# Places modulo 256 bytes: weights at four by turns, normed activations and their sums at three

## The chip, the cores and the metric

The kernel runs on one core of one Trainium2 chip, as one program. The metric is the device time of that program in microseconds, as the median of repeated runs; beside it stands one execution that was recorded instruction by instruction, and everything below that is called a profile or a trace comes from that execution. Times of single instructions are given in nanoseconds (ns).

## The reference

The model is a trunk of two identical layers on one sequence of 512 tokens with 1024 features, in float32:

```python
for l in range(DEPTH):                       # DEPTH = 2
    h = rms_norm(x, ln1[l])
    x = x + mixer_block(h, ...)              # one projection w_in for everything below, then
                                             # four causal mixers, sigmoid gates, w_up_*, w_out
    h = rms_norm(x, ln2[l])
    x = x + swiglu(h, w_ffn_in[l], w_ffn_out[l])

def swiglu(h, w_in, w_out):
    gate, up = jnp.split(h @ w_in, 2, axis=-1)
    return (jax.nn.silu(gate) * up) @ w_out  # 2816 hidden features
```

Nearly all of the arithmetic is in the dense products: the combined projection `w_in`, the four `w_up`, `w_out`, and the two of the feed-forward part. The mixers (forgetting attention, gated linear attention, retention, a state-space scan) work on 64-wide heads and are small beside them.

## The kernel before

**Layout.** Activations are kept transposed: 128 features on the partitions, 512 tokens along a partition, eight such blocks for 1024 features. A product is built of blocks of 128 x 128 weights: the weight block is the stationary operand of a matmul (it is loaded into the array by a weight load, PEld in the profile), the 512 tokens are the moving operand.

**Two parts of every number.** TensorE multiplies a rounded float32 format in one pass. To keep the precision, each operand is split: `split` (lines 210 and 211) lets ScalarE make the rounded part `hi` and VectorE the remainder `lo`. A product of two split operands is three matmuls, hi.hi, hi.lo and lo.hi (`mm3`). So a weight exists as two tiles, `wh` and `wl`; a normed activation as `xh` and `xl` (class `Norm`); what else is projected from is split into tiles named `t` (mixers' outputs, the merged branches) and `f` (the feed-forward activations).

**The weights' stream.** The weights come in slabs of eight blocks (128 x 1024 float32, 512 KB), in the order in which they are used. `load` fetches a slab into a tile `wr` (two buffers), `convert` splits it into `wh` and `wl` (three buffers each), two slabs ahead of their use (`AHEAD`). `half(tag, shift)` makes such a tile 64 elements longer than the data and returns the data's part from element `shift` on. In the stream `shift` is 16 elements, 64 bytes, for every slab. One slab of eight blocks feeds 24 matmuls.

**The feed-forward input product.** Two of its 22 hidden blocks go through the plain way (`group`). The other 20 go in pairs through a seven-product scheme for 2 x 2 blocks (`strassen`), ten pairs (units) per layer, seven products each, 24 matmuls of 256 tokens per product, so 2 x 10 x 7 x 24 = 3,360 matmuls in all. It needs sums and differences of weights and of activations. The weights' sums are made per unit by VectorE from four slabs (`rq`, and one `wr`), split into `wh` and into a tile `l` of its own pool (or, for three of the products, `wl`, made by an accumulating DMA on line 1278). Here `half` is called with `shift` 0. The activations' sums `t1`, `t2`, `t3` stand in six tiles of pool `tq`; a fourth sum and the three plain quarters stand in the tiles of the second norm, `xh` and `xl`. Partial results are kept in tiles `e` (ScalarE copies them out of the accumulators on line 1340, VectorE adds them on line 1344).

**Order.** The order of the instructions on each engine is fixed when the program is built. The change leaves that order as it is on all five engines.

**Places.** A tile's address along the partition, modulo 256 bytes, is called its place here. Pads between the pools set it. In the program as built, the operands of the large groups of matmuls stand at these places:

| matmuls | moving operand, place | stationary operand, place |
|---|---|---|
| 512 tokens, from a norm (2,976 matmuls) | `xh`, `xl`: 192 | `wh`, `wl`: 192 |
| 512 tokens, from `f` (1,056) and `t` (864) | 192 | `wh`, `wl`: 192 |
| 512 tokens, constants (88) | `t`: 192 | `cr`: 128 |
| 256 tokens, seven-product scheme (3,360) | `xh`, `xl`, `t1`, `t2`, `t3`: 192 | `wh`, `wl`, `l`: 128 |
| 256 tokens, values by tokens (384) | `wh`, `wl`: 192 | `xh`, `xl`: 192 |
| 284 tokens, the wide columns (192) | `wh`, `wl`: 192, 48, 160 | `xh`, `xl`: 192 |

The functions that the change touches, and what calls them:

Of the kernel before, what the change touches and what calls it, by code (L numbers as in the profile page):

```python
# [11 lines left out]
F32R = mybir.dt.float32r  # L12
# [6 lines left out]
P = 128  # L19
S = 512  # L20
D = 1024
KD = D // P
# [13 lines left out]
SLAB = 8  # L36
# [11 lines left out]
HK = KD // 2  # L48
H = S // 2
# [82 lines left out]
def trunk(ctx: ExitStack, tc: tile.TileContext, keys, qkeys, xin, pos, wst, wsq, par, ext, cst, out):  # L132
# [7 lines left out]
    bp = ctx.enter_context(tc.tile_pool(name="bp", bufs=1))  # L140
# [7 lines left out]
    def nm(s):  # L148
        uid[0] += 1
        return f"{s}{uid[0]}"  # L150

    def pad(pool, n):
        pool.tile([P, n // 4], F32, tag=nm("pad"), name=nm("pad"))

    def half(tag, shift):
        t = wp.tile([P, SLAB * P + 64], F32R, tag=tag, name=nm(tag))
        return t[:, shift:shift + SLAB * P]

    pools = {}

    def phase(**bufs):
        if not pools:
            for g, n in zip(gap, (192, 64)):
                pad(g, n)
        st = ExitStack()
        pad(st.enter_context(tc.tile_pool(name=nm("gap"), bufs=1)), 64)
        for n, b in bufs.items():
            pools[n] = st.enter_context(tc.tile_pool(name=nm(n), bufs=b, reuse_waits="tile"))
        return st

    def mixers():
        return phase(gp=2, vp=2, bd=1, tp=33)
# [7 lines left out]
    def FT(shape, dtype=F32):  # L180
        return pools["fp"].tile(shape, dtype, tag="f", name=nm("f"))
# [27 lines left out]
    def split(src, hi, lo):  # L209
        A.copy(out=hi, in_=src)  # L210
        V.tensor_tensor(out=lo, in0=src, in1=hi.bitcast(F32), op=ALU.subtract)  # L211
        return hi, lo
# [38 lines left out]
    def halves(n):  # L251
        w = SLAB * P
        return [slice(0, w // 2), slice(w // 2, w)] if n < 2 else [slice(0, w)]

    def convert():
        n = len(ready)
        if n < SLABS:
            hi, lo = half("wh", 16), half("wl", 16)
            for h in halves(n):
                split(raw[n][:, h], hi[:, h], lo[:, h])  # L260
            ready.append((hi, lo))
            raw[n] = None

    def ahead(n):
        while len(ready) < min(SLABS, cap[0], n):
            if len(raw) == len(ready):
                load()
            convert()
# [24 lines left out]
    scope = mixers()  # L293
# [73 lines left out]
    def rstd_of(total, width):  # L367
# [3 lines left out]
        newton(r, total, width, NT())  # L371
        return r

    class Norm:
        def __init__(self, gain):
            self.gain = gain
            self.hi = bp.tile([P, KD, S], F32R, tag="xh", name=nm("xh"))
            self.lo = bp.tile([P, KD, S], F32R, tag="xl", name=nm("xl"))
            self.part = []

        def __getitem__(self, k):
# [51 lines left out]
    def layer(l, n1, scope):  # L433
# [769 lines left out]
        scope.close()  # L1203


        scope = phase(tq=1, ep=8, rp=5, g0=1, lp=2, g1=1, fp=9)
        pad(pools["g0"], 192)
        pad(pools["g1"], 64)

        last = l == DEPTH - 1  # L1210
        tb_ = {n: tuple(pools["tq"].tile([P, HK, H], F32R, tag=n + h, name=nm(n + h)) for h in "hl") for n in ("t1", "t2", "t3")}
        tb_["t4"] = n2.hi[:, :HK, H:], n2.lo[:, :HK, H:]
        tb_["b11"] = n2.hi[:, :HK, :H], n2.lo[:, :HK, :H]
        tb_["b21"] = n2.hi[:, HK:, :H], n2.lo[:, HK:, :H]
# [29 lines left out]
        def strassen(units):  # L1244
            n = len(units)
            st = [{} for _ in units]
            stream = [(0, 1), (0, 2)]
# [7 lines left out]
            def load(u):  # L1255
                for q, (dk, dm) in (("11", (0, 0)), ("12", (HK, 0)), ("21", (0, 1)), ("22", (HK, 1))):
                    if q == "22":
                        t = wp.tile([P, SLAB * P], F32, tag="wr", name=nm("wr"), bufs=2)
                    else:
                        t = pools["rp"].tile([P, SLAB * P], F32, tag="rq", name=nm("rq"))  # L1260
                    j = len(qkeys) // SLAB
                    for base in (0, FFN):
                        qkeys.extend([("w_ffn_in", l, k + dk, base + (units[u] + dm) * P) for k in range(HK)])
                    nc.sync.dma_start(out=t, in_=wsq[j])
                    st[u][q] = t, j

            def sub(o, a, b, op=ALU.subtract):
                V.tensor_tensor(out=o, in0=a, in1=b, op=op)
                return o

            def LT():
                return pools["lp"].tile([P, SLAB * P], F32R, tag="l", name=nm("l"))

            def early(u, p):
                t, j = st[u][OF[p]]
                lo = half("wl", 0)
                A.activation(out=lo, in_=t, func=AF.Copy, scale=-1.0)  # L1277
                G.dma_start(out=lo, in_=wsq[j], accum_op=ALU.add)  # L1278
                st[u]["lo", p] = lo

            def prep(u, p):
                s = st[u]
                hi = half("wh", 0)
                if p in LATE:
                    A.copy(out=hi, in_=s[OF[p]][0])
                    s[p] = hi, s.pop(("lo", p))
                    return
                a11, a12, a21, a22 = (s[q][0] for q in ("11", "12", "21", "22"))
                if p == 6:
                    s1 = wp.tile([P, SLAB * P], F32, tag="wr", name=nm("wr"), bufs=2)  # L1290
                    s["s1"] = sub(s1, a21, a22, ALU.add)
                    sub(a21, a11, a21)
                    sub(a11, s1, a11)
                    s[p] = split(a11, hi, LT())
                    if u + 1 < len(units):
                        load(u + 1)
                    return
                if p == 3:
                    sub(a12, a12, a11)
                t = {5: s["s1"], 7: a21, 3: a12}[p]  # L1300
                s[p] = split(t, hi, LT())

            done_ = {"early": 0, "prep": 0}

# [7 lines left out]
            def begin(i):  # L1312
                if i < 0:
                    if not done_["early"]:
                        load(0)
                    upto("early", -i, early, lambda p: p in LATE)
                    return
                upto("prep", i + 3, prep, lambda p: True)
                upto("early", i + 6, early, lambda p: p in LATE)
# [74 lines left out]
        a, u = FT([P, 2, S]), FT([P, 2, S])  # L1394
# [5 lines left out]
        hi, lo = split(a, FT([P, 2, S], F32R), FT([P, 2, S], F32R))  # L1400
# [46 lines left out]
    for l in range(DEPTH):  # L1447
        n1 = layer(l, n1, scope if l == 0 else mixers())
# [71 lines left out]
```

## Time and profile before

| what | value |
|---|---|
| median of 3 runs | 1731.86 us (1731.65 to 1731.87) |
| the profiled execution, its own time | 1730.43 us |
| its span, first to last instruction | 1728.7 us |
| TensorE matmuls, busy | 1718.3 us, 99% of the span |
| weight loads, busy | 1497.1 us, 87% |
| VectorE | 1212.5 us, 70% |
| ScalarE | 861.3 us, 50% |
| GpSimd | 227.7 us, 13% |
| DMA engines, mean busy | 20% to 60% by stage, 113 GB/s over the span |
| TensorE clock granted | 0.999 of full speed |

A matmul's duration in the trace runs from its start to its modelled end and overlaps the next one's: a matmul of 512 tokens is shown with about 390 ns while the next one starts some 227 ns after it. So the distance between two starts is what counts, and a difference in the mean duration of two groups of the same size is a difference in that distance. The weight load of the next matmul starts a few ns after a matmul's start and runs beside it.

### The profile page before, as it was taken

The numbers are of one execution on the slowest core, as the hardware profiler recorded it, in microseconds if no ns is written. First come the engines' busy times: TensorE is split into PE (matmuls) and PEld (weight loads), VectorE is DVE, ScalarE is ACT, GpSimd is POOL, SyncE is SP. The second block draws the span as 40 slices with busy tenths as digits, with TensorE's granted clock in tenths as the row PEclk, the third lists the DMA queues.
The fourth block names the chain that finished last, engine by engine and source line by source line (L and its number), as shares of the span: only waits on it lengthen the run. The fifth ranks groups of instructions, "written<-read, shape, count | busy, mean of one in ns | idle before, by whom it ended". The sixth has DMA issues, their size and how long they took to land.

```text
span 1728.7 us, 25141 instructions
## 1 busy us (share of the span) xinstructions
PE 1718.3 (99%) x10140; PEld 1497.1 (87%) x10140; DVE 1212.5 (70%) x1683; ACT 861.3 (50%) x1190; POOL 227.7 (13%) x227
## 2 busy tenths in 40 slices
PE   9999999999999999999999999999999999999998
PEld 7878888888888999998988788888888899999998
DVE  5867666768677676675777676767776786766666
ACT  5425543555457555464544254435553574655543
POOL 2032110022101010100010322200221010101010
PEclk9999999999999999999999999999999999999999
DMA  5222222222235656565333222223222365665653
GB/s 202 101 74 73 75 85 74 85 88 76 92 98 162 174 135 180 132 182 121 87 98 111 73 74 74 85 75 96 76 84 86 98 188 154 150 167 137 180 107 102
DMA packets 54693, 195.00 MB, mean 113 GB/s; under 512 B 6064, under 2 KB 6448, under 8 KB 54576
## 3 DMA queue, kind: packets, MB, share of 16 engines
q1 hardware_dynamic: 45072, 160.45, 29.1%
q0 software_dynamic: 8640, 31.46, 10.2%
q8 instruction: 79, 1.29, 0.3%
q10 hardware_dynamic: 864, 1.48, 0.2%
q14 instruction: 38, 0.31, 0.1%
HBM read 191.27 MB, written 2.10 MB: 112 GB/s over the span
## 4 chain that ended last, share of the span: by engine, by line
PE 96%; DVE 1%; ACT 1%; DMA 1%; issue 0%; SPq 0%; DVEq 0%
PE mm L196 65%; PE mx L196 31%; PE mx L1070 0%; DMA x<-in_x_dram 0%; DMA wr<-in_wst_dram 0%; ACT wh L210 0%; DVE wl L211 0%; ACT t L234 0%; PE mx L670 0%; DVE t L364 0%; ACT L229 0%; DVE t L827 0%; ACT g L234 0%; DVE t L1159 0%; PE mx L862 0%
## 5 line engine op out<-in xcount | busy, mean ns | idle before, releaser
L210 ACT CAST wh<-wr 128x1024 fp32r<-128x1024 f32 (+1 forms) x240 | 249.4, 1041 | 382.0 <-PE mm L196 233.7
L196 PE MATMUL mm<-xh,wh 128*128 128x512 f32 (+1 forms) x1184 | 429.6, 363 | 0.9 <-DVE t L1159 0.9
L196 PE MATMUL mm<-xh,wl 128*128 128x512 f32 (+1 forms) x1184 | 428.6, 362 | 0.0
L196 PE MATMUL mm<-xl,wh 128*128 128x512 f32 (+1 forms) x1184 | 427.7, 361 | 0.0
L211 DVE TENSOR_TENSOR wl<-wr,wh 128x1024 fp32r<-128x1024 f32 (+1 forms) x220 | 279.6, 1272 | 121.2 <-ACT wh L210 119.4
L196 PEld LDWEIGHTS mm<-xh,wh 128*128 128x128 f32 x1184 | 222.4, 188 | 35.3 <-DVE t L1159 1.8
L196 PEld LDWEIGHTS mm<-xh,wl 128*128 128x128 f32 x1184 | 222.5, 188 | 34.8 <-issue 1.5
L196 PEld LDWEIGHTS mm<-xl,wh 128*128 128x128 f32 x1184 | 222.3, 188 | 33.7 <-issue 1.1
L196 PE MATMUL mm<-t,wh 128*128 128x512 f32 x448 | 140.2, 392 | 0.0
L196 PE MATMUL mx<-xl,wh 128*128 128x256 f32 (+1 forms) x448 | 139.1, 311 | 0.0
L196 PE MATMUL mx<-xh,wh 128*128 128x256 f32 (+1 forms) x448 | 136.7, 312 | 2.4 <-ACT wh L210 2.4
L1278 POOL DMA_DIRECT2D wl<-in_wsq_dram x60 | 51.9, 864 | 528.3 <-ACT wl L1277 421.5
L196 PE MATMUL mx<-f,wh 128*128 128x512 f32 x352 | 108.3, 390 | 0.0
L196 PE MATMUL mm<-f,wh 128*128 128x512 f32 x352 | 106.0, 390 | 0.0
L196 PEld LDWEIGHTS mm<-t,wh 128*128 128x128 f32 x448 | 83.2, 188 | 17.1
L211 DVE TENSOR_TENSOR l<-rq,wh 128x1024 fp32r<-128x1024 f32 x60 | 73.2, 1220 | 34.2 <-ACT wh L210 19.2
L196 PEld LDWEIGHTS mx<-xh,wh 128*128 128x128 f32 x448 | 84.0, 188 | 8.7 <-ACT wh L210 3.5
L196 PE MATMUL mx<-xh,wl 128*128 128x256 f32 (+1 forms) x288 | 91.2, 328 | 0.0
L196 PEld LDWEIGHTS mx<-xl,wh 128*128 128x128 f32 x448 | 84.0, 188 | 5.0
L196 PE MATMUL mm<-t,wl 128*128 128x512 f32 x224 | 87.4, 390 | 0.0
L210 ACT CAST wh<-rq 128x1024 fp32r<-128x1024 f32 x60 | 63.0, 1050 | 44.2 <-PE mm L196 21.7
L196 PEld LDWEIGHTS mm<-f,wh 128*128 128x128 f32 x352 | 66.1, 188 | 13.7
(275 smaller groups left out, 3466.9 us busy)
## 6 DMA issues: line engine op xcount, KB each, us to landing
wr<-in_wst_dram SPq DMA_DIRECT2D x216, 512.0 KB, 3.5
rq<-in_wsq_dram SPq DMA_DIRECT2D x60, 512.0 KB, 5.5
wl<-in_wsq_dram POOLq DMA_DIRECT2D x60, 512.0 KB, 7.1
wr<-in_wsq_dram SPq DMA_DIRECT2D x20, 512.0 KB, 7.1
out_dram<-x SPq DMA_DIRECT2D x8, 256.0 KB, 2.0
x<-in_x_dram SPq DMA_DIRECT2D x3, 512.0 KB, 6.8
wr<-in_wst_dram SPq DMA_DIRECT2D x4, 256.0 KB, 5.6
x<-in_x_dram SPq DMA_DIRECT2D x2, 256.0 KB, 4.6
```

The lines of the kernel that those rows point to most:

```text
L196: T.matmul(o, lhsT=l, rhs=r, start=start, stop=stop, skip_group_check=True)
L210: A.copy(out=hi, in_=src)
L211: V.tensor_tensor(out=lo, in0=src, in1=hi.bitcast(F32), op=ALU.subtract)
L1278: G.dma_start(out=lo, in_=wsq[j], accum_op=ALU.add)
```

## The change

Four edits, all of which only move data along the partition:

- `convert`: the slab's parts stand at `n % 4 * 16` elements instead of always 16, so that slab after slab their place is 128, 192, 0, 64 by turns.
- `early`, `prep`, `LT`: the same in the seven-product scheme, by the product's number in `stream`; the tiles `l` grow by 64 elements for it.
- `Norm`: the tiles `xh`, `xl` grow by 32 elements, and the data starts at element 0, 16, 32, 32 for the four norms of the program. Since `xl` lies behind the longer `xh`, its place moves by another 128 bytes.
- the sums `t1`, `t2`, `t3` get pads behind them, and pool `ep` (tiles `e`) goes from 8 buffers to 6.

In the program as built, the places become:

| operand | before | with the change |
|---|---|---|
| `wh`, `wl` of the stream | 192 | 128, 192, 0, 64 by turns |
| `wh`, `wl`, `l` in the seven-product scheme | 128 | 128, 192, 0, 64 by turns |
| `xh` / `xl`, the four norms in turn | 192 / 192 | 192 / 64, 0 / 128, 64 / 192, 64 / 192 |
| `t1`, `t2`, `t3` (both parts) | 192 | 192, 0, 64 |
| `f`, `t`, `cr`, `rq`, `wr`, `e`, `n` | 192, 192, 128, 192, 128, 192, 192 | the same |

The order of the instructions on each engine stays the same, and so do the waits of TensorE and VectorE. Twelve of ScalarE's 120 copies into `e` have one more wait, for VectorE. On SyncE, four of the first loads of weights into `rq` have other waits, for work of the stage before; one wait less stands on GpSimd.

```diff
@@ convert
-            hi, lo = half("wh", 16), half("wl", 16)
+            hi, lo = half("wh", n % 4 * 16), half("wl", n % 4 * 16)
@@ Norm
+    norms = [0]
+
     class Norm:
         def __init__(self, gain):
             self.gain = gain
-            self.hi = bp.tile([P, KD, S], F32R, tag="xh", name=nm("xh"))
-            self.lo = bp.tile([P, KD, S], F32R, tag="xl", name=nm("xl"))
+            at = (0, 16, 32, 32)[norms[0]]
+            norms[0] += 1
+            self.hi = bp.tile([P, KD * S + 32], F32R, tag="xh", name=nm("xh"))[:, at:at + KD * S].rearrange("p (k s) -> p k s", k=KD)
+            self.lo = bp.tile([P, KD * S + 32], F32R, tag="xl", name=nm("xl"))[:, at:at + KD * S].rearrange("p (k s) -> p k s", k=KD)
@@ layer, after the mixers
-        scope = phase(tq=1, ep=8, rp=5, g0=1, lp=2, g1=1, fp=9)
+        scope = phase(tq=1, ep=6, rp=5, g0=1, lp=2, g1=1, fp=9)
...
-        tb_ = {n: tuple(pools["tq"].tile([P, HK, H], F32R, tag=n + h, name=nm(n + h)) for h in "hl") for n in ("t1", "t2", "t3")}
+        tb_ = {}
+        for n in ("t1", "t2", "t3"):
+            tb_[n] = tuple(pools["tq"].tile([P, HK, H], F32R, tag=n + h, name=nm(n + h)) for h in "hl")
+            pad(pools["tq"], 128 if n == "t3" else 64)
@@ strassen
             def LT():
-                return pools["lp"].tile([P, SLAB * P], F32R, tag="l", name=nm("l"))
+                return pools["lp"].tile([P, SLAB * P + 64], F32R, tag="l", name=nm("l"))
 
             def early(u, p):
                 t, j = st[u][OF[p]]
-                lo = half("wl", 0)
+                lo = half("wl", stream.index((u, p)) % 4 * 16)
...
             def prep(u, p):
                 s = st[u]
-                hi = half("wh", 0)
+                shift = stream.index((u, p)) % 4 * 16
+                hi = half("wh", shift)
...
-                    s[p] = split(a11, hi, LT())
+                    s[p] = split(a11, hi, LT()[:, shift:shift + SLAB * P])
...
-                s[p] = split(t, hi, LT())
+                s[p] = split(t, hi, LT()[:, shift:shift + SLAB * P])
```

## The prediction

> **What bounds the kernel now.** I read the page first: how busy each engine is, and the chain of waits that ended last. Then what TensorE itself waits for.
>
> ```profile
> PE 1718.3 (99%) x10140; PEld 1497.1 (87%) x10140; DVE 1212.5 (70%) x1683; ACT 861.3 (50%) x1190; POOL 227.7 (13%) x227
> PE 96%; DVE 1%; ACT 1%; DMA 1%; issue 0%; SPq 0%; DVEq 0%
> PE mx L196 <- ACT wh L210: 2.4, 3, 1.1
> PE mm L196 <- POOL t L320: 1.4, 1, 1.4
> PE mx L196 <- DVE t L211: 1.2, 2, 0.6
> PE mm L196 <- DVE t L1159: 0.9, 2, 0.5
> ```
>
> TensorE fills the chain, and its four kinds of wait come to 5.9 us. No other engine decides the time: only the distance from one matmul's start to the next can. A busy share of 99% does not say that this distance is the least possible, so the next views are of that distance. The chain of waits has long pieces of matmuls of 512 tokens back to back, and the groups by form give each kind's mean duration:
>
> ```profile
> 505.38 21.76 PE mm L196 x96
> L196 PE MATMUL mm<-xh,wh 128*128 128x512 f32 x864 | 340.2, 394 | 0.9 <-DVE t L1159 0.9
> L196 PE MATMUL mx<-f,wh 128*128 128x512 f32 x352 | 108.3, 390 | 0.0
> L196 PE MATMUL mm<-t,wh 128*128 128x512 f32 x448 | 140.2, 392 | 0.0
> L196 PE MATMUL mx<-t,wh 128*128 128x512 f32 x128 | 39.7, 389 | 0.0
> L196 PE MATMUL mx<-t,cr 128*128 128x512 f32 x96 | 34.7, 397 | 0.0
> ```
>
> 21.76 us over 96 is 226.7 ns. The groups of 512 tokens whose operands both stand at place 192 are near the 389 to 390 ns that belong to this spacing. The one group whose stationary operand, the constant `cr`, stands at 128 has 397 ns. The matmuls of 256 tokens are the other large kind:
>
> ```profile
> 1411.00:1444.00 33.00, 33.00 (x294) 1.00 0.82 210
> 1480.00:1513.00 33.00, 33.00 (x282) 1.00 0.76 183
> L196 PE MATMUL mx<-xl,wh 128*128 128x256 f32 x32 | 8.8, 276 | 0.0
> L196 PE MATMUL mx<-xl,wh 128*128 128x256 f32 x24 | 6.7, 279 | 0.0
> L196 PE MATMUL mm<-t3h,wh 128*128 128x256 f32 x160 | 44.5, 279 | 0.0
> 1411.20 0.28 PE L196 MATMUL mx<-xh,wl 128*128 128x256 f32 x1
> 1411.43 0.28 PE L196 MATMUL mx<-xl,wh 128*128 128x256 f32 x1
> 553.07 0.28 PE L196 MATMUL mx<-xh,wl 128*128 128x256 f32 x1
> 553.54 0.28 PE L196 MATMUL mx<-xh,wh 128*128 128x256 f32 x1
> ```
>
> The first two rows are two windows of 33 us, both inside the seven-product scheme of the second layer, with the same instructions at the same places and the same granted clock (1.00): 294 matmuls in one, 282 in the other. The next two rows are one group of matmuls in about these windows, 276 and 279 ns, and the fifth the mean of a group over the whole run: the slower spacing rules. The last four, from the timeline (start times), give the spacing: two matmuls in 0.23 us, and four in 0.47 us in the first layer. I use 33 us and the counts to keep the ratio (294 / 282 is 4% ) and 113.3 and 117.8 ns for the two: 226.7 / 2 is 113.3, and 113.3 x 1.04 is 117.8. So a stream of matmuls can settle into one of two spacings, 4.5 ns apart, without any engine waiting.
>
> **The change part by part.** No instruction is added, removed or moved, so every term is a price per matmul: what the spacing does when places differ. I call the place of the moving operand minus the place of the weights that load meanwhile, modulo 256, the *relation*. Today it is 0 for the large products of 512 tokens and 64 in the seven-product scheme. From the table of places, with the change all four relations (0, 64, 128, 192) are about equally common in both, and they alternate: `xh` and `xl` stand 128 apart, so in the products of a norm the relation jumps within every group of three.
>
> What a relation other than 0 costs at 512 tokens is shown only where `cr` comes between:
>
> ```profile
> 317.16 0.40 PE L196 MATMUL mx<-t,cr 128*128 128x512 f32 x1
> 318.09 0.39 PE L196 MATMUL mm<-xl,wh 128*128 128x512 f32 x1
> 251.49 0.40 PE L196 MATMUL mx<-t,cr 128*128 128x512 f32 x1
> ...
> 256.12 0.39 PE L196 MATMUL mm<-xh,wl 128*128 128x512 f32 x1
> ```
>
> One `cr` among weights at 192 (first two rows, four matmuls apart): 0.93 us where 4 x 226.7 is 0.907, so one change of place and back costs some 21 to 23 ns, after which the stream is at 226.7 again. Where a `cr` comes every two or three matmuls (the other two rows, twenty matmuls apart): 4.63 us, 231.5 ns each, 4.8 ns over. I take 5 ns as the price of a matmul in a stream whose relation keeps changing.
>
> Term 1, 512 tokens from a norm, 2,976 matmuls, and from `f` and `t`, 1,920. Relation 0 costs nothing more, relation 64 the 5 ns of its nearest rows. No row shows 128 and 192: from below they cost nothing (they may settle as 0 does; there is hardly anything to gain, since today's groups stand at 389 to 394 ns where 389 is the settled value), from above 5 ns again; I take half, 2.5 ns, as nothing favours one end. The mean over four is (0 + 5 + 2.5 + 2.5) / 4 = 2.5 ns: 2,976 x 2.5 = 7.4 us and 1,920 x 2.5 = 4.8 us, together +12.2 us. The bounds are 0 and 4,896 x 5 = 24.5 us.
>
> Term 2, the seven-product scheme, 3,360 matmuls at 117.8 ns today. The other end is shown by the values by tokens, whose relation is 0 at 256 tokens:
>
> ```profile
> 166.30 0.28 PE L196 MATMUL mm<-wh,xh 128*128 128x256 f32 x1
> ...
> 167.14 0.28 PE L196 MATMUL mm<-wl,xh 128*128 128x256 f32 x1
> L196 PE MATMUL mm<-wl,xh 128*128 128x256 f32 x128 | 36.5, 285 | 0.0
> ```
>
> Seven matmuls in 0.84 us are 120 ns each. So relation 0 is 120, relation 64 is 117.8, and the two unknown ones lie between the settled 113.3 and 120; I take the middle, 116.7. The mean, (120 + 117.8 + 116.7 + 116.7) / 4 = 117.8, is what is there today: 0 us. The bounds: all at 113.3, 3,360 x -4.5 = -15 us; all at 120, 3,360 x 2.2 = +7.4 us.
>
> Term 3, the values by tokens, 384 matmuls now at 120: at a mean of 117.8 they win 384 x 2.2 = 0.8 us; -0.8 us.
>
> Term 4, the pool `ep` with 6 buffers:
>
> ```profile
> L1340 ACT COPY e<-mm x120: 349/372/405, 548.6 to 1696.2; 128x256 f32<-128x256 f32 x120
> L1344 DVE TENSOR_TENSOR f<-mx,e x120: 414/418/425, 562.6 to 1701.0; 128x256 f32<-128x256 f32 x120
> ```
>
> Twelve of the 120 copies now wait for VectorE's addition of six tiles earlier. The tightest are the tiles that are added after a unit's product 3 and written again after the next unit's product 6: product 4 and product 6 lie between, 2 x 24 x 117.8 = 5.7 us of TensorE work against two additions of 0.42 us. So it is hidden, 0. Without that cover ScalarE's next weight splits would be queued behind the copy, for 12 x 0.42 = 5 us at the most. The loads into `rq` with other waits go out at the same place of SyncE's queue:
>
> ```profile
> 524.26 3.03 SPq L1264 DMA_DIRECT2D rq<-in_wsq_dram  x5
> rq<-in_wsq_dram SPq DMA_DIRECT2D x60, 512.0 KB, 5.5
> L1277 ACT ACTIVATE wl<-rq x2: 1055/1057/1059, 534.9 to 541.3; 128x1024 fp32r<-128x1024 f32 x2
> ```
>
> Five issues from 524.3 to 527.3, landing 5.5 us later, first read at 534.9: about 2 us to spare for the last of the five, more for the first. Their new waits are for the stage before; 0.
>
> Sum: 12.2 + 0 - 0.8 = +11.4 us. The profiled execution took 1730.43 us (1728.7 of span and 1.7 around it): 1741.8. The median of the runs is 1.4 us above that execution: 1743.3, **1743 us**.
>
> **A rule that speaks against all of it.** The rows first: the same matmuls at the same clock come at 113.3 or 117.8 ns, and a single `cr` at another place costs 21 ns. The Trainium skill, "TensorE: Matmul & The Clock Gate", Part 2, "Step-by-step: what each phase is for", says that TensorE has two independent read ports into the on-chip memory, so loading the next weights takes nothing from the running matmul. By it places would not matter and the sum would be 0 instead of 11.4 us; that is the second rival below. The trace does not agree, in so far as `cr` at 128 stands at 397 ns beside 389 for the same moving tiles; a reason for `cr` other than its place is not excluded by the rows.
>
> **The rivals.**
> *Faster: the seven-product scheme settles.* In 1411 to 1444 it ran at 113.3 ns for some 290 matmuls. If relations 128 and 192 (half of the matmuls) settle there at once, 1,680 x 4.5 = 7.6 us are won, and if a change of relation lets the others slip into it too, 15 us: 1731.9 - 15 = 1717, and about 1724 for half. It needs the products of 512 tokens to stay settled: it decides once Term 1 is under 7 us. For it: the faster spacing exists at unchanged places. Against: the means of whole groups, 279 where 276 is settled, say that it is rare today, and alternating relations disturb a stream more than constant ones.
> *No change.* Places do not matter, or what is won and lost cancels: 1732. For it: nothing else in the program moves. Against: the `cr` rows.
> *Much slower.* Every relation other than 0 keeps the stream unsettled, and the jumps spoil relation 0 as well: 4,896 x 5 = 24.5 us, and part of the +7.4 us at 256 tokens: about 1760. For it: the stretch 251.5 to 256.1, in which only eight of the twenty matmuls are `cr` and still the mean is 231.5. Against: after one disturbance the stream settles within four matmuls.
>
> **How the numbers follow.** The forecast, slower by some 5 to 20 us (1737 to 1752), has 0.50; much slower 0.13; no change 0.15; faster 0.22. So slower by over 0.2% has 0.63, within 0.2% (3.5 us, about what runs of this kernel can tell from no change) 0.15, faster 0.22. The likeliest case's own range is 1737 to 1752. For 8 in 10 the range has to reach into both other sides: 1722, which leaves out the lower part of the faster case (0.08), to 1758, which leaves out the upper part of the much slower one (0.08).
>
> **What would show it.** Right: no new waits of TensorE, the same counts; the groups of 512 tokens from `xh` and `xl` at 395 to 397 ns instead of 392 to 394, those of `f` at 392 instead of 390; the long pieces of 96 matmuls at some 22.0 us instead of 21.76. The groups of 256 tokens in the seven-product scheme spread between 276 and 282 ns by product, with a mean near 279. Wrong: the 512 groups stay at today's means (then Term 1 is 0 and the sign hangs on Term 2); the 256 groups fall to 276 (faster); or the mean spacing per matmul rises by 9 ns and more, which no row above allows for a whole stream. A new wait of ScalarE on VectorE before line 1340 that ends at TensorE would show Term 4 wrong.

## The result and the profile after

| | before | with the change |
|---|---|---|
| median of 3 runs | 1731.86 us | 1747.71 us (1747.61 to 1748.14) |
| profiled execution, its own time | 1730.43 us | 1747.71 us |
| its span | 1728.7 us | 1746.0 us |

The ratio is 1.0093, with a 95% interval of 1.0070 to 1.0115: 15.85 us slower. The forecast was 1743 us, slower. The two profiled spans lie 17.3 us apart, because the profiled execution of the kernel before was 1.4 us under its median; the ledger below is of these two executions. One execution of a later experiment (relation 192 in the scheme) took 1807.27 us at a granted clock of 0.897 and is left out of every comparison.

The 1.4 us have a likely source. The seven-product scheme runs in eight long stretches without a pause, four per layer, of some 309 to 503 matmuls each. In the profiled execution of the kernel before, one of them (the first window of the prediction) ran at 113.3 ns instead of 117.8: 309 x 4.45 ns = 1.4 us. Since only one execution of each kernel was traced, it is not shown that its other executions lack this.

First the page of the changed kernel, engines and chain, and then what TensorE waits for there (microseconds, times, longest):

```profile
PE 1735.4 (99%) x10140; PEld 1498.7 (86%) x10140; DVE 1215.3 (70%) x1683; ACT 861.5 (49%) x1190; POOL 226.5 (13%) x227
PE 97%; ACT 1%; DVE 1%; issue 0%; DMA 0%; ACTq 0%; DVEq 0%
```

```profile
PE mx L196 <- ACT wh L210: 3.0, 3, 1.7
PE mm L196 <- POOL t L320: 1.4, 1, 1.4
PE mx L196 <- DVE t L211: 1.0, 2, 0.5
PE mm L196 <- DVE t L1163: 0.8, 2, 0.4
```

The same 10,140 matmuls, and the same four kinds of wait with 6.2 us instead of 5.9. The busy time of PE is 17.1 us longer, and that is nearly the whole difference of the spans. So the matmuls themselves come at a greater distance. The groups by form of the changed kernel (busy time, mean ns of one):

```profile
L196 PE MATMUL mm<-xh,wh 128*128 128x512 f32 x864 | 343.4, 397 | 0.8 <-DVE t L1163 0.8
L196 PE MATMUL mx<-f,wh 128*128 128x512 f32 x352 | 109.4, 393 | 0.0
L196 PE MATMUL mm<-t,wh 128*128 128x512 f32 x448 | 141.7, 395 | 0.0
L196 PE MATMUL mx<-t,wh 128*128 128x512 f32 x128 | 40.2, 393 | 0.0
L196 PE MATMUL mx<-t,cr 128*128 128x512 f32 x96 | 34.7, 397 | 0.0
L196 PE MATMUL mm<-t2h,wh 128*128 128x256 f32 x160 | 44.8, 283 | 0.0
L196 PE MATMUL mm<-t3h,wh 128*128 128x256 f32 x160 | 44.7, 280 | 0.0
L196 PE MATMUL mm<-wl,xh 128*128 128x256 f32 x128 | 36.2, 283 | 0.0
```

The groups of 512 tokens whose places changed have gained 3 to 4 ns (394 to 397, 390 to 393, 392 to 395, 389 to 393); the constant `cr`, whose places did not change, has its 397 ns as before. The groups of 256 tokens shown moved by 1 to 2 ns, those of the scheme up and the values by tokens down (before: 281, 279 and 285).

One place shows the mechanism without any averaging. The chain of the changed kernel has the same long piece of 96 matmuls as before, which is four slabs of 24 matmuls on the moving tiles `t` at place 192:

```profile
510.34 22.13 PE mm L196 x96
```

It took 21.76 us before. The four slabs stand at 64, 128, 192 and 0, and the timeline shows each of them. Each slab has eight matmuls with `wl`, one in three; the rows are the first and the eighth of each slab, 21 matmuls apart (start us, duration us):

```profile
510.64 0.40 PE L196 MATMUL mm<-t,wl 128*128 128x512 f32 x1
...
515.52 0.39 PE L196 MATMUL mm<-t,wl 128*128 128x512 f32 x1
516.22 0.39 PE L196 MATMUL mm<-t,wl 128*128 128x512 f32 x1
...
521.02 0.40 PE L196 MATMUL mm<-t,wl 128*128 128x512 f32 x1
521.72 0.39 PE L196 MATMUL mm<-t,wl 128*128 128x512 f32 x1
...
526.49 0.39 PE L196 MATMUL mm<-t,wl 128*128 128x512 f32 x1
527.18 0.40 PE L196 MATMUL mm<-t,wl 128*128 128x512 f32 x1
...
532.08 0.39 PE L196 MATMUL mm<-t,wl 128*128 128x512 f32 x1
```

4.88, 4.80, 4.77 and 4.90 us for 21 matmuls: 232.4 ns at relation 128, 228.6 at relation 64, 227.1 at relation 0 and 233.3 at relation 192, one after the other in the same product, with the same moving tiles, the same instructions and no wait. (The relation is, as in the prediction, the place of the moving operand minus the place of the weights that load meanwhile, modulo 256.)

For the whole run I joined the address of every matmul's operands in the built program with its start in the trace, and took the distance to the next start, less the settled value (226.67 ns at 512 tokens, 113.33 at 256; gaps with a wait of over 25 ns are left out). I call that the surplus. Its sums, in microseconds:

| surplus | before | with the change | difference |
|---|---|---|---|
| 512 tokens (4,896 matmuls) | 5.0 | 20.8 | +15.8 |
| 256 tokens (3,744 matmuls) | 16.3 | 18.1 | +1.8 |

15.8 + 1.8 = 17.6, against the 17.3 us between the spans. Of the +1.8, 1.4 is the stretch at 113.3 ns that the changed kernel's profile lacks. And by relation, mean surplus in ns, for the products of `f` and `t` (among `t` those with the constants `cr`), whose relation is constant within a slab:

| with the change, 512 tokens | 0 | 64 | 128 | 192 |
|---|---|---|---|---|
| `f` | 1.2 | 2.7 | 5.7 | 6.5 |
| `t` | 3.0 | 3.3 | 5.5 | 6.3 |

Before, with everything at relation 0, `f` had 0.7, `t` 1.1 and the products of a norm 1.0.

### The profile page after: what moved, and what is told of

Read it like the earlier page. It is cut to its first block, busy times and chain, and to the rows that moved or that the text cites. A ratio compares the mean times of both kernels' runs of the same rounds, so it can differ in the third digit from the quotient of the medians.

```text
span 1746.0 us, 25149 instructions
## 1 busy us (share of the span) xinstructions
PE 1735.4 (99%) x10140; PEld 1498.7 (86%) x10140; DVE 1215.3 (70%) x1683; ACT 861.5 (49%) x1190; POOL 226.5 (13%) x227
## 4 chain that ended last, share of the span: by engine, by line
PE 97%; ACT 1%; DVE 1%; issue 0%; DMA 0%; ACTq 0%; DVEq 0%
PE mm L196 65%; PE mx L196 31%; PE mx L1074 0%; ACT wh L210 0%; DVE wl L211 0%; ACT L229 0%; DMA x<-in_x_dram 0%; PE mx L674 0%; ACT xh L234 0%; DVE t L364 0%; ACT n L234 0%; ACT g L234 0%; DVE t L1163 0%; ACT t L234 0%; PE mx L866 0%
## 5 line engine op out<-in xcount | busy, mean ns | idle before, releaser
L196 PEld LDWEIGHTS mm<-f,wh 128*128 128x128 f32 x352 | 66.2, 188 | 14.7
```

The lines of the kernel that those rows point to most:

```text
L196: T.matmul(o, lhsT=l, rhs=r, start=start, stop=stop, skip_group_check=True)
```

## The experiments

Each kernel was compared with the kernel before on the same chip. The theory under test is that of the prediction: the time of a matmul in a stream depends on the relation, and nothing else in the change matters. Its main rival: the price is not of the relation but of its changes, at each slab and within each group of three.

**Four parts, each alone.** First only the stream's slabs by turns:

```diff
@@ convert
-            hi, lo = half("wh", 16), half("wl", 16)
+            hi, lo = half("wh", n % 4 * 16), half("wl", n % 4 * 16)
```

> Only the weights of the stream stand at four places by turns; norms, sums and the seven-product scheme as before. By the theory that the price belongs to the relation (moving place minus the place of the weights loading meanwhile), with the prices of the trace with the change for matmuls from f and t (spacing above the settled one at relation 0, 64, 128, 192: 1.2, 2.7, 5.7, 6.5 ns; today about 1.0), 4,896 matmuls of 512 tokens cost 3.0 ns more each: +15 us, and the four relations show these prices again. By the rival that only a change of place costs (about 22 ns each) and a constant relation settles again: 204 slabs, +4 to 5 us, and the spacing inside a slab goes back to 226.7 ns after four or five matmuls, whatever the relation.

Then only the places of the norms (with `ep=6`, without which the longer tiles have no room):

```diff
@@ Norm
+            at = (0, 16, 32, 32)[norms[0]]
...
-            self.hi = bp.tile([P, KD, S], F32R, tag="xh", name=nm("xh"))
+            self.hi = bp.tile([P, KD * S + 32], F32R, tag="xh", name=nm("xh"))[:, at:at + KD * S].rearrange("p (k s) -> p k s", k=KD)
```

> Only the normed activations are moved (and the pool of partial results has 6 buffers). The stream's weights stay at 192, so in layer 1 xh has relation 0 and xl 128, in layer 2 the other way round. Relation theory: half of the 2,976 matmuls from a norm go from 1.0 to 5.7 ns: +7 us; a little either way in the seven-product scheme. Rival of changes: the relation jumps twice in every three matmuls, so the stream never settles: 2,976 x 4 to 5 ns, +12 to 15 us, with relation 0 and 128 at the same mean.

Then only the weights of the seven-product scheme (`early`, `prep` and `LT` as in the change, and `ep=6`):

```diff
@@ strassen
-                lo = half("wl", 0)
+                lo = half("wl", stream.index((u, p)) % 4 * 16)
...
-                hi = half("wh", 0)
+                shift = stream.index((u, p)) % 4 * 16
+                hi = half("wh", shift)
```

> Only the weights of the seven-product scheme stand at four places by turns, one per product. Both theories: between the prices of the trace with the change for t1 (5.8, 4.7, 5.4, 4.5 ns above the settled spacing at relation 0, 64, 128, 192; today 4.1): 3,360 x 1.0 = +3 us; at most +8 us (all at 120 ns), and -5 us if relations 128 and 192 settle.

Then only the activations' sums, with `ep=6`:

```diff
@@ layer, after the mixers
-        scope = phase(tq=1, ep=8, rp=5, g0=1, lp=2, g1=1, fp=9)
+        scope = phase(tq=1, ep=6, rp=5, g0=1, lp=2, g1=1, fp=9)
...
+            pad(pools["tq"], 128 if n == "t3" else 64)
```

> Only the sums t1, t2, t3 stand at three places, and the pool of partial results has 6 buffers instead of 8. Relation theory: t2 has relation 128, t3 192, 480 matmuls each: within 1 us of no change. The 6 buffers cost nothing: no new wait of TensorE. A time more than 3 us above would say that the buffers cost something after all.

| alone | median | before, same chip | difference | ratio, 95% interval |
|---|---|---|---|---|
| stream's slabs | 1746.39 | 1731.89 | +14.5 us | 1.0085 (1.0056 to 1.0114) |
| norms | 1741.06 | 1731.89 | +9.2 | 1.0052 (1.0029 to 1.0075) |
| scheme's weights | 1733.11 | 1731.89 | +1.2 | 1.0007 (0.9996 to 1.0018) |
| sums `t1` to `t3` | 1731.49 | 1731.89 | -0.4 | 0.9996 (0.9985 to 1.0007) |

The stream alone already has the groups of the whole change, here by form:

```profile
L196 PE MATMUL mm<-xh,wh 128*128 128x512 f32 x864 | 342.7, 397 | 0.8 <-DVE t L1159 0.8
L196 PE MATMUL mx<-f,wh 128*128 128x512 f32 x352 | 109.3, 393 | 0.0
```

With the norms alone the products of a norm stand there too, and those of `f`, whose places did not move, are at their old value:

```profile
L196 PE MATMUL mm<-xh,wh 128*128 128x512 f32 x864 | 343.1, 397 | 0.8 <-DVE t L1163 0.8
L196 PE MATMUL mx<-f,wh 128*128 128x512 f32 x352 | 108.2, 389 | 0.0
```

The four differences sum to 24.5 us, and the whole change gives 15.85: the parts are not independent. Turning the stream spreads the 512-token matmuls over all four relations; if the norms stand elsewhere too, the spread is over the same four, only in another order. The mean surplus of the products of a norm is 4.2 ns with the stream alone and 4.3 with the whole change.

The norms alone gave +9.2 us, between the theory's +7 and the rival's +12 to +15, and neither describes them. In the first layer `xh` keeps relation 0 and `xl` goes to 128; in the second `xh` goes to 128 and `xl` keeps 0. (The first layer's feed-forward norm, 96 matmuls, has 64 and 192.) `xh` moves in two matmuls of three. Here is one of its groups in the first layer (window 0 to 870 us) and in the second (870 us to the end), before:

```profile
L196 PE MATMUL mm<-xh,wh 128*128 128x512 f32 x432 | 170.3, 394 | 0.5 <-DVE t L1159 0.5
L196 PE MATMUL mm<-xh,wh 128*128 128x512 f32 x432 | 169.9, 393 | 0.5 <-DVE t L1159 0.5
```

and with the norms moved:

```profile
L196 PE MATMUL mm<-xh,wh 128*128 128x512 f32 x432 | 172.1, 398 | 0.4 <-DVE t L1163 0.4
L196 PE MATMUL mm<-xh,wh 128*128 128x512 f32 x432 | 171.0, 396 | 0.4 <-DVE t L1163 0.4
```

The group rises by 4 ns where its own relation is still 0, and by 3 ns where it is 128. Over all products of a norm the mean surplus is 4.8 ns in the first layer and 2.8 in the second. The prices that the relations have when they are constant (measured below, about 1 ns at 0 and 6 at 128) would give (1 + 6 + 1) / 3 = 2.7 and (6 + 1 + 6) / 3 = 4.3, the other way round. So where the relation changes from one matmul to the next, a matmul does not simply pay the price of its own relation; no run here takes this apart.

In the sums' experiment `t2` (relation 128) has 283 ns and `t3` (relation 192) 279, beside 281 and 279 before, and the total stays. Six buffers in `ep` cost nothing that can be told from no change.

In the stream's experiment there are changes of relation only at every 24th matmul, and still +14.5 us came where the theory had +15 and the rival +4 to +5. So the changes are not what costs most. They do cost something: in this run, the first ten gaps after a return to relation 0 are together some 21 ns over.

**Constant relations at 512 tokens.** To price each relation alone, the stream's weights were put at one other place for all slabs. There is no change of relation left, except at the constants. `shift` is 0 for relation 64, 48 for 128 and 32 for 192:

```diff
@@ convert
-            hi, lo = half("wh", 16), half("wl", 16)
+            hi, lo = half("wh", 0), half("wl", 0)
```

> Everything as before, but the stream's weights stand at place 128 throughout: every matmul of 512 tokens has the constant relation 64, and no place changes from slab to slab. Relation theory, by the prices of the run with the stream's turns (2.6 to 3.4 ns at 64, 1.0 today): 4,896 x 2 ns = +9 to 10 us, less some 2 us in the values by tokens, whose relation becomes 192: about +7 to 8 us. Rival of changes: a constant relation settles, 0 to +1 us.

> The stream's weights stand at place 64 throughout, so the relation of the 4,896 matmuls of 512 tokens is a constant 128, the only relation at 512 tokens not yet run by itself. If the prices read with turns (5.6 ns at relation 128, within slabs of 24 matmuls) are steady prices of the relation, each of the 4,896 matmuls pays 5.6 ns instead of about 0.9: +23 us. If they are in part the price of a change of relation at each slab, a constant 128 settles lower, as a constant 64 stayed at 2.4: then clearly under +18 us, and 0 if it settles like relation 0. The values by tokens come to relation 128 at 256 tokens and stay at 119.9 ns or a little less (6.4 against 6.7 ns over 113.3: 0 us); the seven-product scheme is not touched (within 4 us, by how many stretches settle). So 1755 us for steady prices.

> The same with the stream's weights at place 0: constant relation 192 at 512 tokens. Relation theory (6.4 ns at 192): 4,896 x 5.4 ns = +26 us, less about 1 us in the values by tokens: +25 us, with a spacing that alternates between 231 and 236 ns. Rival of changes: 0 to +1 us.

| relation at 512 tokens, constant | difference | ratio, 95% interval | surplus of `f`, `t`, norm (ns) | surplus sum, 512 / 256 tokens (us) |
|---|---|---|---|---|
| 0 (kernel before) | | | 0.7, 1.1, 1.0 | 5.0 / 16.3 |
| 64 | +2.2 us | 1.0017 (1.0005 to 1.0028) | 2.3, 2.4, 2.4 | 12.6 / 11.3 |
| 128 | +23.5 | 1.0136 (1.0119 to 1.0153) | 6.5, 6.0, 5.9 | 29.3 / 17.3 |
| 192 | +26.2 | 1.0149 (1.0119 to 1.0178) | 6.6, 6.5, 6.6 | 31.7 / 16.9 |

The piece of 96 matmuls that took 21.76 us before, in the chains of the three kernels, in this order 64, 128, 192:

```profile
507.04 21.97 PE mm L196 x96
```

```profile
513.25 22.31 PE mm L196 x96
```

```profile
514.90 22.40 PE mm L196 x96
```

The mean of the four constants, (21.76 + 21.97 + 22.31 + 22.40) / 4 = 22.11, is the 22.13 us of the changed kernel, in which each of the four slabs of this piece stands at one of the four relations. The group of `f` tells the same in the kernel at 192; it was at 390 ns before:

```profile
L196 PE MATMUL mm<-xh,wh 128*128 128x512 f32 x864 | 344.4, 399 | 0.8 <-DVE t L1159 0.8
L196 PE MATMUL mx<-f,wh 128*128 128x512 f32 x352 | 110.4, 396 | 0.0
```

So the price belongs to the relation and is paid by each matmul for as long as the relation lasts; a constant one does not settle away. At 128 and 192 the theory's +23 and +25 us came as +23.5 and +26.2. At 64 the 512-token matmuls cost 12.6 - 5.0 = +7.6 us where +9 to 10 was expected, and yet the kernel was only 2.2 us slower: 5.0 us came back at 256 tokens where 2 was expected, so that the forecast of +7 to +8 us was missed. Two windows of 33 us inside the scheme of this kernel show where (window, length, then busy time of PE, PEld, VectorE, ScalarE and GpSimd, each with its number of instructions, granted clock, DMA share, GB/s):

```profile
630.00:663.00 33.00, 33.00 (x294) 33.00 (x293) 21.81 (x25) 22.88 (x35) 4.62 (x6) 1.00 0.86 213
720.00:753.00 33.00, 33.00 (x283) 33.00 (x282) 21.29 (x25) 22.30 (x33) 3.94 (x5) 1.00 0.86 205
```

The scheme's places are those of the kernel before. But two of its eight long stretches ran at 113.3 ns, where before one did. In the seven traces here that have the scheme at the relation of the kernel before (64), 3 of 56 long stretches ran so; each is worth 1.4 to 2.2 us. That fits the spread of this kernel's eight executions, 1733.06 to 1738.66 us. The values by tokens, whose relation became 192, went to 113.4 ns in three of their four stretches:

```profile
L196 PE MATMUL mm<-wl,xh 128*128 128x256 f32 x128 | 35.9, 280 | 0.0
```

**Relation or place?** Here the first gap's pad grows by 64 bytes, so that everything but the constants moves by 64 together and only the places change:

```diff
@@ phase
-            for g, n in zip(gap, (192, 64)):
+            for g, n in zip(gap, (256, 64)):
```

> One pad at the start is 64 bytes longer, so that weights, norms, sums and every other tile behind it move by 64 bytes together; all relations stay, but each place is another one. Relation theory: no change, within 1 us (or the small differences of which spacing the seven-product scheme happens to settle in, up to 2 us). A rival by which the place of the weights itself counts, not the relation: the stream's weights at place 0 would cost what they cost with the turns, +20 us and more.

1732.29 us against 1731.87, ratio 1.0000 (0.9989 to 1.0011). Two groups of it:

```profile
L196 PE MATMUL mx<-f,wh 128*128 128x512 f32 x352 | 108.3, 390 | 0.0
L196 PE MATMUL mx<-t,cr 128*128 128x512 f32 x96 | 35.0, 400 | 0.0
```

All large groups keep their 390 to 394 ns at other places. Only `cr`, against which the others moved (relation 128 instead of 64), goes from 397 to 400. It is the relation that counts, not the place.

One part of the definition is not shown: that the weights which load meanwhile count, and not the matmul's own. Within a slab both stand at the same place, and where they differ the traces point both ways. At the 41 borders from relation 0 to 192 in the stream's run, the last gap ahead of the border has 0.3 ns over and the next one 8.5, as if a matmul's own weights counted. In the run just shown, the 53 gaps of a norm's matmul ahead of a `cr`, which loads at relation 128, have 5.3 ns over, as if the loading ones did.

**Constant relations in the seven-product scheme.** The scheme's weights at one other place throughout, with the longer `l` tiles and `ep=6`. The shift is 16 for relation 0, 48 for 128 and 32 for 192; shown is the last:

```diff
@@ strassen
-                lo = half("wl", 0)
+                lo = half("wl", 32)
...
-                hi = half("wh", 0)
+                shift = 32
+                hi = half("wh", shift)
```

> As before, but the weights of the seven-product scheme at place 192 throughout: constant relation 0 at 256 tokens. Relation theory: the 120 ns of the values by tokens, which have that relation today: 3,360 x 2.2 ns = +7 us. Rival (which spacing comes is chance at each restart, the relation has no part in it): stretches at 113.3 and 117.8 ns as at relations 64 and 192, within 2 us of before.

> The same with the weights of the seven-product scheme at place 64: constant relation 128. Relation theory, by the prices of the runs with turns (5.1 to 5.8 ns above the settled spacing at 128, 4.4 today): 3,360 x 1.0 = +3 us. Rival: within 2 us of before.

> Everything as before, but the weights of the seven-product scheme stand at place 0 throughout: constant relation 192 there (6 buffers in the pool of partial results). Relation theory: 192 had the lowest price of the four at 256 tokens in the earlier runs (2.6 to 4.5 ns above the settled spacing, against 4.0 to 4.7 at 64): 3,360 x -0.5 to -1.5 ns = -2 to -5 us; -15 us if a constant 192 settles altogether. Rival: the spacing in the scheme is set by chance at the restart after each pause, not by the relation: within 2 us of before.

| relation in the scheme, constant | difference | ratio, 95% interval | surplus sum, 256 tokens (us) |
|---|---|---|---|
| 64 (kernel before) | | | 16.3 |
| 0 | +6.9 us | 1.0040 (1.0025 to 1.0055) | 25.0 |
| 128 | +7.0 | 1.0039 (1.0024 to 1.0054) | 24.3 |
| 192 | -1.3 | 0.9991 (0.9979 to 1.0002) | 16.3 |

Windows of 30 us in the kernels at 0 and at 192 (two of it, in different units):

```profile
730.00:760.00 30.00, 30.00 (x252) 30.00 (x251) 21.64 (x25) 20.68 (x30) 3.46 (x4) 1.00 0.79 181
```

```profile
553.00:583.00 30.00, 30.00 (x267) 30.00 (x267) 23.59 (x28) 23.18 (x35) 3.43 (x4) 1.00 0.78 210
730.00:760.00 30.00, 30.00 (x257) 30.00 (x256) 23.66 (x27) 21.76 (x32) 3.45 (x4) 1.00 0.69 157
```

At relation 0 all eight long stretches stand at 120 ns, as the theory had it (+7 us). At 128 they stand at 118.7 to 120.0, where +3 us was expected: a miss. The prices of the runs with turns were too low for it, and so was the middle between 113.3 and 120 that the prediction had put in for the unseen relation: the value is at the dear end. At 192 one stretch of eight (the first window above) ran at 113.4 ns and seven at 117.8, just as at 64: the gain of 2 to 5 us that was expected did not come, and its interval includes no change.

**A version that is faster than both.** What the prices suggest: keep the products of 512 tokens at relation 0, give the constants relation 0 too, and take the values by tokens, at relation 0 the dearest there is for 256 tokens, to 192. Eight slabs feed the values by tokens:

```diff
@@ phase
-            for g, n in zip(gap, (192, 64)):
+            for g, n in zip(gap, (128, 64)):
@@ convert
-            hi, lo = half("wh", 16), half("wl", 16)
+            at = 0 if n % 109 in (25, 26, 41, 42) else 16
+            hi, lo = half("wh", at), half("wl", at)
@@ ahead of the constants
+    pad(cp, 64)
```

> An attempt at a faster version from the prices found: as before, but the eight slabs of the values by tokens stand at place 128 (relation 192 at 256 tokens, where the run with the stream at 128 had 113.4 ns in three of four stretches), and the constants cr at 192, so that a cr among weights no longer changes the relation. Relation theory: 384 x -5 ns = -2 us, and some sixty bumps of 21 ns less, -1.3 us: -3 us, 1729. Rival (chance at each restart): 0 to -1 us.

1728.79 us against 1731.94, ratio 0.9982 (0.9972 to 0.9991): 3.15 us faster. The groups and a window in the values by tokens:

```profile
L196 PE MATMUL mm<-wl,xh 128*128 128x256 f32 x128 | 35.8, 279 | 0.0
L196 PE MATMUL mx<-t,cr 128*128 128x512 f32 x96 | 34.2, 392 | 0.0
```

```profile
166.00:172.00 6.00, 6.00 (x54) 5.96 (x53) 5.90 (x10) 3.02 (x6) 1.28 (x4) 1.00 0.29 87
```

The same window in the kernel before:

```profile
166.00:172.00 6.00, 6.00 (x51) 5.96 (x51) 5.91 (x9) 2.60 (x7) 1.21 (x4) 1.00 0.25 87
```

279 ns instead of 285, and 392 instead of 397; the window has 54 matmuls instead of 51. All four stretches of values by tokens ran at 113.4 to 113.8 ns. By the prices, 384 x 6.2 ns = 2.4 us came from them, and the surplus of the 512-token matmuls fell from 5.0 to 4.0 us. No long stretch of the scheme ran at 113.3 ns in the profile of this version.

## Why the prediction was right, and where its terms were wrong

**What bounds the kernel** was read rightly: the busy share of 99% hid the loss, which lay in the distance between starts. No other engine took part; the waits of TensorE changed by 0.3 us.

**Term 1** (+12.2 us, bounds 0 to 24.5) is the whole result, as the forecast said, and measured +15.8 in the profiled execution. The direction, the count of matmuls and the kind of cause (a price per matmul, set by the relation) were right; the four prices behind the mean were not. Put in were 0, 5, 2.5 and 2.5 ns for relations 0, 64, 128 and 192. Measured by constant relations: some 1, 2.4, 6 and 6.6. The step that failed is the reading of the `cr` rows: their 4.8 ns came from a stream whose relation keeps changing, and the step took it for the price of relation 64. A constant 64 costs half of it, and the two relations for which the middle was taken are at or over the upper bound of 5 ns (5.0 and 5.6 over today's 1 ns). One price was too high and two were too low, so that the sum came near is in part luck. Put into the same sum, the measured prices give (1 + 2.4 + 6 + 6.6) / 4 = 4.0 ns, less the 1 ns that is there today, 4,896 x 3.0 = 14.7 us. For the 1,920 matmuls from `f` and `t` that is the mechanism. For the 2,976 from a norm it is a mean that came out: with alternating relations a matmul does not pay the price of its own, as the norms' experiment shows layer by layer.

**Term 2** (0, bounds -15 to +7.4): alone +1.2 us, within what can be told from no change. The prices here were wrong in the same way (128 dear, not 116.7; 192 like 64), and again the mean stayed near the right place, which is luck too.

**Term 3** (-0.8 us): the values by tokens did gain; the group `wl`,`xh` went from 285 to 283 ns. Terms 2 and 3 together were forecast at -0.8 and measured at +1.8 us, 1.4 of it the stretch that stood at 113.3 ns in the profile before.

**Term 4** (0): right as far as the runs can tell; `ep=6` with the sums moved gave -0.4 us, and no new wait stands at TensorE.

**The rivals.** *Faster*, by the scheme settling at 113.3 ns with alternating relations: no long stretch of the changed kernel ran there, so it fell. But the other spacing is real and came in single stretches at relations 64 and 192 held constant. *No change*: it fell with the constants, +26.2 us from one shift of 64 bytes. By the rule that was cited for it (the Trainium skill, "TensorE: Matmul & The Clock Gate", Part 2, "Step-by-step: what each phase is for", two independent read ports) that shift, as the prediction reads it, would give 0; the trace does not agree. *Much slower*, about 1760: its assumption, that every relation other than 0 costs 5 ns and that jumps spoil relation 0, was too dark for 64. The mean of the constants leaves 0.02 us of the piece of 96 for its jumps. With the norms alone, the jumps within groups of three do spoil relation 0 in the first layer, as this rival had it (`xh`, at relation 0, has 4.2 ns over). But in the second layer relation 128 comes cheaper than it is alone (3.7 ns for `xh`), so that the mean of both layers, 3.8 ns, is near the (1 + 6) / 2 = 3.5 of the constants; no run shows why. The argument against this rival, that a stream settles within four matmuls after a disturbance, was short: in the stream's run it takes about ten.

**The signs** named ahead: 395 to 397 ns for the groups from `xh` and `xl` (the largest groups came at 397, 396 and 394), 392 for `f` (393), pieces of 96 at some 22.0 us (22.13), and 276 to 282 with a mean near 279 for the groups of the seven-product scheme: they came at 280 to 283, with no group near 276.

## What to carry to other kernels

Where TensorE is busy all the time, compare the distance between starts in several stretches of equal instructions: a few ns of difference at the same clock and without waits are a loss that the busy share does not show. In this kernel it was set by the addresses of the moving operand and of the weights, modulo 256 bytes; only differences that are multiples of 64 bytes were run. One constant shift of all weights prices a relation in one run, and the best relation has to be found for each width of matmul by itself. A mean that comes out right can hide parts that are wrong: split it by layer or by stretch before calling it explained.

## What the runs showed of the hardware that was not expected

- **The price by relation differs by width.** In ns over the settled spacing: at 512 tokens 0 costs about 1, 64 costs 2.4, 128 costs 6 and 192 costs 6.6; at 256 tokens 0 costs 6.7, 128 costs 5.4 to 6.7, and 64 and 192 either 4.4 or nothing. These hold where the relation stays the same over a slab or longer.
- **Two spacings at one and the same place.** At 256 tokens and relation 64 or 192 a stretch of several hundred matmuls runs wholly at 117.8 or wholly at 113.3 ns, with the same instructions, order, places and granted clock (the two windows with 294 and 283 matmuls). At relations 0 and 128 held constant, no stretch ran at 113.3 ns. What chooses is open: in the traces a stretch keeps the spacing that it begins with, and the busy time of the other engines and the DMA share in these windows are nearly alike (0.86 in both). No experiment set it on purpose.
- **Most of the prices fit fractions of one step.** This is arithmetic on the starts, not a tested rule. The settled gaps of 226.67 and 113.33 ns are 34 and 17 times 6.667 ns, which is also what separates 120 from 113.33. At relation 192 the gaps at 512 tokens go 235, 231, 236, 231, with a mean of 233.3: one step more for every matmul. At relation 64 they go 232, 226, 229: one step more for every three. At 256 tokens 120 ns is one step more for each, and 117.8 two for every three. The 5.9 to 6.5 ns of relation 128 fit no such simple fraction. Why time is lost in this pattern was not shown.
